# A written VectorE order for the expert loop, with gathered rows used a block later and the low half of the key rows made on VectorE

## The chip, the core and the metric

The kernel runs on one core of a Trainium2 chip, as one launch. The metric is device microseconds of one execution, from the start of the program to its end. The core has five engines that run side by side, each in the order of its own queue: TensorE (PE; its weight loads are shown apart as PEld), VectorE (DVE), ScalarE (ACT), GpSimd (POOL) and SyncE (SP), which here only issues DMA transfers. Engines wait for each other through semaphores.

## The reference

Two layers work on 512 tokens of width 1024 in float32. The first has chunked attention beside a state-space mixer, then attention over a memory of 256 rows; the second has dilated and differential attention. Each ends with the same kind of feed-forward part, a mixture of 16384 experts of one row each, and the change is in that part alone:

```python
def block(xb):                                   # 128 tokens
    q = (xb @ w_q).reshape(PEER_BLOCK, PEER_HEADS, 2, PEER_QDIM // 2)
    s = jnp.einsum('thsd,hsnd->thsn', q, sub_keys)
    sv, si = lax.top_k(s, PEER_TOPK)
    cand = sv[:, :, 0, :, None] + sv[:, :, 1, None, :]
    cidx = si[:, :, 0, :, None] * PEER_KEYS + si[:, :, 1, None, :]
    top, pos = lax.top_k(cand, PEER_TOPK)        # 16 experts for each of 8 heads
    e = jnp.take_along_axis(cidx, pos, axis=-1)
    g = jax.nn.softmax(top, axis=-1)
    act = gelu(jnp.einsum('thkd,td->thk', u_tab[e], xb))
    return jnp.einsum('thk,thkd->td', g * act, v_tab[e])
```

Each token thus uses 128 experts: for each, the dot product of a row of the table U (the key rows) with the token, its gelu times a gate, and that number times a row of the table V (the value rows), summed.

## The kernel before

Both layers call the same function `peer`; the first call has a side job, the second none. It treats the four token tiles of 128 in two ways.

**Three tiles are dense.** For them the gates of all 16384 experts are written out as a matrix (in device memory, `Gd`), and all experts are run as plain products in 128 blocks of 128 experts. For a block e, `pa` is the product of the key rows with the 384 tokens (24 matmuls of 384 columns), `ga` its gelu; `w` is `ga` times the block's gates, and `y` collects w times the value rows (18 matmuls of 512 columns into six accumulators). To keep float32 accuracy, each operand is split into a high half (a cast on ScalarE: `uh`, `vh`, `wh`) and a low half (the original minus the high half: `ul`, `vl`, `wl`), and three products stand for one. Key rows are loaded to `ur` and value rows to `vr`, 512 KB per block each, by SP; gates to `gbuf` for four blocks at a time.

**The fourth tile is gathered.** Row by row, for each of its 128 slots k, GpSimd issues an indirect DMA that fetches for each token its own key row (`urow`, L1229), and VectorE multiplies it with the token and sums (L1230, into `act`). Each 16 slots, ScalarE takes the gelu and VectorE multiplies with the gates (L1233, L1234). 32 slots later the value row is fetched (`vrow`, L1241) and added to `acc` with its weight (L1243). Both kinds of row have a pool of three buffers.

**The loop.** Products `pa` run 28 blocks ahead (`NA`): 28 of them are made before the loop, in the stages of routing and of writing the gates. Pass e of the loop emits: the load of `vr`; `vh` (L1262) and `vl` (L1263); `w`, `wh`, `wl` (L1267 to L1269); then `emit_A(e + 28)` (load of `ur`, `uh` L1099, `ul` L1105, `pa` L1112 to L1115, its gelu L1117); then a share of the list `ev` of the gathered tile's steps; then the matmuls of `y` (L1293 to L1295). From pass 100 on there are no `pa` products left and no gathers. There, in the first call only, the side job runs: the modulation of the second layer (three rows of it, 8 weight tiles `war` of 512 KB each, summed into `am` by VectorE, L823 and L825), two steps in each pass; and GpSimd makes `vl` in place of VectorE in passes 100 to 119. At pass 120 the gathered tile is finished.

**What sets the order.** The program is not run in the order in which it is written: a scheduler orders each engine's instructions when the kernel is compiled, by its own estimate of when each could start, and places the semaphores. `with tc.manual_schedule(engines={...})` takes this away: the instructions inside it, on the engines named, keep the order in which they are written. Before, that is so for GpSimd alone, around `emit_A` and the steps of `ev`. Low and high halves of values and weights, `vr`, `ur`, `uh` and `ul` have two buffers each, so work on a buffer of block e can start when block e-2 has let it go.

Of the kernel before, what the change touches and what calls it, by code (L numbers as in the profile page):

```python
# [8 lines left out]
F32 = mybir.dt.float32  # L9
# [14 lines left out]
def build(tc, I, out, dbg=None, stop=None):  # L24
# [28 lines left out]
    def rsqrt(ssq, n, scale, nm, eps=EPS):  # L53
        """1 / sqrt(ssq * scale + eps) for a [128, n] tile."""
# [24 lines left out]
    def transpose_split(src, ncol, hi, lo, dst, psum=None):  # L79
        """src [128, ncol*128] -> hi/lo[:, k, dst] for each 128-column chunk k."""  # L80
# [13 lines left out]
    def ssq_of(src, junk, nm):  # L94
        """sum of squares along the free axis on the scalar engine"""
        s = sm.tile([src.shape[0], 1], F32, name=nm, tag="ssq")
        A.activation(out=junk, in_=src, func=AF.Square, accum_out=s)
        return s
# [6 lines left out]
    def load_w(W, k, c0, cn, pool=None, e=V):  # L105
        """rows of chunk k of a weight matrix, as high and low halves"""
# [23 lines left out]
    def proj(hiT, loT, W, K, c0, cn, evac, tiles=range(NT), pool=None):  # L130
        """token-major product: for each token tile, psum[128, cn] = h @ W[:, c0:c0+cn]"""
# [16 lines left out]
    def keep_w(pool, W, K, c0, cn=512, last=0, e=V):  # L148
        """a block of weight columns on chip, for products of one token tile after the other"""
# [12 lines left out]
    def proj_rows(hiT, loT, ws, evac, then):  # L162
        """all token tiles in turn; then(t) follows two tiles behind"""
# [7 lines left out]
    # token order of everything after the first mixing: row p of tile r is token 4 p + r  # L171
# [6 lines left out]
    # =====================================================================  # L178
    # block 1: norm, input projection
    # =====================================================================  # L180
# [43 lines left out]
    def head_proj(pool, hi, lo, W, c0, nh, hd, tiles, finish, first=None, wait=False):  # L224
        """nh heads of width hd divided by their root mean square; finish(t, heads, scale)"""
# [92 lines left out]
    def cmul(o_r, o_i, a_r, a_i, b_r, b_i, pool, shape, conj_b=False, e=V):  # L318
        """o = a * b (or a * conj b)"""
# [22 lines left out]
    # powers a^0 .. a^8  # L342
# [14 lines left out]
    # c a^n: real part and negated imaginary part  # L357
# [16 lines left out]
    # unit phases e^{i Theta j}, Theta = 8 theta, and the decay of a chunk  # L374
# [37 lines left out]
    def coefficients():  # L412
        s5x = ExitStack()
        s5t = s5x.enter_context(tc.tile_pool(name="s5t", bufs=1, side="right"))
        # chunk-input coefficients, transposed to [(s, c), pair, (g2, p)]
# [12 lines left out]
        # block-Toeplitz matrices [(s, c_in), g, (t, c_out)], two groups of a pair at a time  # L428
# [94 lines left out]
    def norm_T(xt, gain, hi, lo, sl, pool, inplace=False, two=False):  # L523
        """rmsnorm of a [128, 1024] tile with gain, transposed and split"""
# [218 lines left out]
    def softmax_row(ps, n, z, pool, tag="pe"):  # L743
        """exp(scores - max) with its sum"""
# [43 lines left out]
    def modulation(rows, pool, psum, tags, ptag, on_pool):  # L788
        """rows of the modulation; yields after each block of 128 x 1024 weights"""
# [57 lines left out]
    EV = 100  # L847
# [6 lines left out]
    def queries(qp, Wq, hi, lo):  # L854
        """loads, halves and products of the 128-column blocks of the query weights"""
# [31 lines left out]
    def peer_route(rw, query, keysT, crep, E, GT, ahead, also, first):  # L887
        """expert indices (as float) and gates, [128, tile, 128 slots]

        Step l of 16 is one half of one head's query; the candidates of a head are  # L890
        looked up in the steps of the next head, and products of the first expert
        blocks run between the steps' products."""
# [23 lines left out]
        def top16(src, work, vals, idx, tiles):  # L916
            """the 16 largest of src[:, t] with their places, in order"""
# [152 lines left out]
    def peer(keysT_d, U, UT, Vt, front, finish, nm, side=None, also=None, then=None):  # L1070
# [49 lines left out]
        def emit_A(e):  # L1120
            a_dma(e)
            a_hi(e)
            a_lo(e)
            a_mm(e)
# [742 lines left out]
```

## Time and profile before

| | |
|---|---|
| three runs | 4092.52, 4095.1, 4101.62 us, median 4095.1 |
| span of the profiled execution, first to last instruction | 4090.4 us |
| PE busy | 3876.8 us, 95% |
| VectorE, GpSimd, ScalarE busy | 3004.6, 2145.8, 1654.8 us |
| the first expert loop | about 970 to 1960 us, its tail without `pa` from about 1807 on |
| the second expert loop | about 3116 to 4082 us, its tail from about 3958 on |

Lines such as L1263 are those of the kernel before. The profiled execution gives its span and not a time of its own beside it. PE's busy share counts pipelined matmuls, so the number of matmuls in a stretch tells more of its pace than the share does.

### The profile page before, as it was taken

The numbers are of one execution on the slowest core, as the hardware profiler recorded it, in microseconds if no ns is written. First come the engines' busy times: TensorE is split into PE (matmuls) and PEld (weight loads), VectorE is DVE, ScalarE is ACT, GpSimd is POOL, SyncE is SP. The second block draws the span as 40 slices with busy tenths as digits, with TensorE's granted clock in tenths as the row PEclk, the third lists the DMA queues.
The fourth block names the chain that finished last, engine by engine and source line by source line (L and its number), as shares of the span: only waits on it lengthen the run. The fifth ranks groups of instructions, "written<-read, shape, count | busy, mean of one in ns | idle before, by whom it ended". The sixth has DMA issues, their size and how long they took to land. (4 is left out here: it accounts for less than half of the span.)

```text
span 4090.4 us, 53234 instructions
## 1 busy us (share of the span) xinstructions
PE 3876.8 (95%) x19062; PEld 3370.2 (82%) x19062; DVE 3004.6 (73%) x5440; ACT 1654.8 (40%) x2567; POOL 2145.8 (52%) x1353
## 2 busy tenths in 40 slices
PE   6999998899999999989899988999899999999999
PEld 5777788899899999877777766788899899989887
DVE  8456489884787778777756566689884788878765
ACT  3454432454333333323444567332454333333333
POOL 3000057655777777754424433257655777776740
PEclk8999999999999999999999989999999999999999
DMA  3333132236898889986222323332237898888874
GB/s 112 99 111 106 52 113 79 101 134 230 302 319 320 315 311 315 318 275 221 90 81 57 93 75 100 102 114 79 98 134 250 299 322 314 311 306 308 299 254 150
DMA packets 330057, 784.31 MB, mean 192 GB/s; under 512 B 32048, under 2 KB 148864, under 8 KB 326400
## 3 DMA queue, kind: packets, MB, share of 16 engines
q1 hardware_dynamic: 252608, 499.86, 36.4%
q0 software_dynamic: 77184, 281.05, 19.5%
q8 instruction: 150, 2.46, 0.2%
q14 instruction: 115, 0.94, 0.1%
HBM read 722.98 MB, written 56.65 MB: 191 GB/s over the span
## 5 line engine op out<-in xcount | busy, mean ns | idle before, releaser
L1105 POOL TENSOR_TENSOR ul<-ur,uh 128x1024 fp32r<-128x1024 f32 x256 | 676.5, 2643 | 378.0 <-ACT uh L1099 259.5
L1112 PE MATMUL pa<-phi,uh 128*128 128x384 f32 x2048 | 695.5, 340 | 0.8 <-ACT ga L1117 0.8
L1113 PE MATMUL pa<-plo,uh 128*128 128x384 f32 x2048 | 694.8, 339 | 0.0
L1294 PE MATMUL y<-vl,wh 128*128 128x512 f32 x1536 | 606.2, 395 | 26.1 <-DVE vl L1263 22.4
L1295 PE MATMUL y<-vh,wl 128*128 128x512 f32 x1536 | 609.2, 397 | 11.3 <-DVE wl L1269 11.3
L1293 PE MATMUL y<-vh,wh 128*128 128x512 f32 x1536 | 603.8, 394 | 1.3 <-ACT wh L1268 1.2
L1243 DVE SCALAR_TENSOR_TENSOR acc<-vrow,act,acc 128x1024 f32<-128x1024 f32 x256 | 392.3, 1532 | 196.6 <-DMA vrow<-in_expert_v_dram,ei 99.5
L1230 DVE SCALAR_TENSOR_TENSOR urow<-urow,hgat 128x1024 f32<-128x1024 f32 x256 | 392.0, 1534 | 172.0 <-DMA urow<-in_peer_u_dram,ei 85.5
L1268 ACT CAST wh<-w 128x384 fp32r<-128x384 f32 x256 | 131.2, 513 | 736.0 <-PE y L1294 483.8
L1099 ACT CAST uh<-ur 128x1024 fp32r<-128x1024 f32 x256 | 269.3, 1052 | 382.9 <-PE pa L1113 149.2
L1115 PE MATMUL pa<-phi,ul 128*128 128x384 f32 x2048 | 402.5, 339 | 18.0 <-POOL ul L1105 17.9
L1112 PEld LDWEIGHTS pa<-phi,uh 128*128 128x128 f32 x2048 | 389.0, 190 | 10.0 <-ACT ga L1117 1.1
L1113 PEld LDWEIGHTS pa<-plo,uh 128*128 128x128 f32 x2048 | 389.1, 190 | 9.6
L1263 DVE TENSOR_TENSOR vl<-vr,vh 128x1024 fp32r<-128x1024 f32 x236 | 353.4, 1498 | 34.6 <-DMA ur<-in_peer_uT_dram 16.2
L1115 PEld LDWEIGHTS pa<-phi,ul 128*128 128x128 f32 x2048 | 362.0, 190 | 19.9 <-POOL ul L1105 19.9
L1206 PE MATMUL pgg<-oh,oh 128*128 128x128 f32 x1536 | 374.3, 421 | 4.4 <-DVE oh L1198 3.9
L1206 PEld LDWEIGHTS pgg<-oh,oh 128*128 128x128 f32 x1536 | 369.9, 337 | 7.1 <-issue 5.3
L1294 PEld LDWEIGHTS y<-vl,wh 128*128 128x128 f32 x1536 | 290.5, 189 | 93.5 <-DVE vl L1263 32.3
L1295 PEld LDWEIGHTS y<-vh,wl 128*128 128x128 f32 x1536 | 290.5, 189 | 85.0 <-DVE wl L1269 22.5
L1293 PEld LDWEIGHTS y<-vh,wh 128*128 128x128 f32 x1536 | 290.8, 189 | 55.5 <-ACT wh L1268 1.7
L77 DVE TENSOR_TENSOR wl<-wr,wh 128x512 fp32r<-128x512 f32 (+1 forms) x276 | 198.9, 729 | 148.9 <-ACT wh L76 148.8
L1200 POOL TENSOR_TENSOR oh<-oha,ohb 128x1024 f32<-128x1024 f32 x72 | 218.2, 3033 | 143.9 <-PE pgg L1206 104.5
(539 smaller groups left out, 7694.7 us busy)
## 6 DMA issues: line engine op xcount, KB each, us to landing
vr<-in_peer_v_dram SPq DMA_DIRECT2D x128, 512.0 KB
ur<-in_peer_uT_dram SPq DMA_DIRECT2D x128, 512.0 KB
vr<-in_expert_v_dram SPq DMA_DIRECT2D x128, 512.0 KB
ur<-in_expert_uT_dram SPq DMA_DIRECT2D x128, 512.0 KB
gbuf<-Gd SPq DMA_DIRECT2D x64, 768.0 KB
Gd<-stg SPq DMA_DIRECT2D x24, 1920.0 KB
wr<-in_w_in_dram SPq DMA_DIRECT2D x104, 256.0 KB
war<-in_w_ada_dram SPq DMA_DIRECT2D x24, 512.0 KB
```

The costliest lines, as they stand in the source:

```text
L1099: A.copy(out=uh, in_=ua[e])
L1105: G.tensor_tensor(out=ul, in0=raw, in1=uh.bitcast(F32), op=OP.subtract)
L1112: T.matmul(pa, uh[:, k, :], hi[:, k, 0:NDT], start=(k == 0), stop=False)
L1113: T.matmul(pa, uh[:, k, :], lo[:, k, 0:NDT], start=False, stop=False)
L1115: T.matmul(pa, ul[:, k, :], hi[:, k, 0:NDT], start=False, stop=(k == 7))
L1206: T.matmul(pg[:, j, :], oh2[:, :, 4 * q + j], oh1[:, :, 4 * q + j], start=True, stop=True)
L1230: V.scalar_tensor_tensor(out=row, in0=row, scalar=1.0, in1=hg_, op0=OP.mult, op1=OP.mult, accum_out=act[:, k:k + 1])
L1243: V.scalar_tensor_tensor(out=acc, in0=vrow.pop(k - 2), scalar=act[:, k - 2:k - 1], in1=acc, op0=OP.mult, op1=OP.add)
L1263: (G if side and EV <= e < EW else V).tensor_tensor(out=vl, in0=vr, in1=vh.bitcast(F32), op=OP.subtract)
L1293: T.matmul(y[t][c], wh[:, ts], vh[:, cs_], start=(e_ == 0), stop=False)
L1294: T.matmul(y[t][c], wh[:, ts], vl[:, cs_], start=False, stop=False)
L1295: T.matmul(y[t][c], wl[:, ts], vh[:, cs_], start=False, stop=(e_ == 127))
```

## The change

- The part under `manual_schedule` now holds VectorE's instructions too and begins earlier, so that VectorE's steps of a pass come in the written order: `w`, `vl`, `wl`, the uses of gathered rows, then `ul` of block e + 28. ScalarE's casts stand inside but stay with the scheduler; they are emitted as `wh`, `vh`.
- `emit_A(e + NA, V)` makes `ul` on VectorE instead of GpSimd in the loop's 100 passes. The 28 blocks before the loop keep GpSimd.
- A step of `ev` is now a pair of a fetch and a use. A pass uses the rows that the pass before fetched (`due`), and then fetches its own share. Before, a key row was used in the step that fetched it, and a value row two steps later. The 16-slot gelu is part of the last use of its 16. `ev` has 256 entries where it had 266, over the same 99 passes.
- `vl` is made on VectorE in all passes; GpSimd's share in passes 100 to 119 of the first call is gone.
- Comments are removed. Pools and buffer counts stay.

```diff
-        def a_lo(e):
+        def a_lo(e, eng=G):
             raw, uh = ua[e]
             ul = ub.tile([128, 8, 128], F32R, name="ul", tag="ul")
-            G.tensor_tensor(out=ul, in0=raw, in1=uh.bitcast(F32), op=OP.subtract)
+            eng.tensor_tensor(out=ul, in0=raw, in1=uh.bitcast(F32), op=OP.subtract)
...
-        def g_u(k):
-            row = gw.tile([128, 1024], F32, name="urow", tag="row")
-            G.indirect_dma_start(out=row, out_offset=None, in_=U, in_offset=bass.IndirectOffsetOnAxis(ap=ei[:, TL, k:k + 1], axis=0))
+        rows_ = {}
+
+        def u_in(k):
+            rows_[0, k] = gw.tile([128, 1024], F32, name="urow", tag="row")
+            G.indirect_dma_start(out=rows_[0, k], out_offset=None, in_=U, in_offset=bass.IndirectOffsetOnAxis(ap=ei[:, TL, k:k + 1], axis=0))
+
+        def u_use(k):
+            row = rows_.pop((0, k))
             V.scalar_tensor_tensor(out=row, in0=row, scalar=1.0, in1=hg_, op0=OP.mult, op1=OP.mult, accum_out=act[:, k:k + 1])
+            if k % 16 == 15:
+                k0 = k - 15
+                A.activation(out=act[:, k0:k0 + 16], in_=act[:, k0:k0 + 16], func=AF.Gelu)
+                V.tensor_tensor(out=act[:, k0:k0 + 16], in0=act[:, k0:k0 + 16], in1=GT[:, TL, k0:k0 + 16], op=OP.mult)
...
         ev = []
-        for k in range(128 + 34):
+        for k in range(128 + 32):
             if k < 128:
-                ev.append((g_u, k))
-                if k % 16 == 15:
-                    ev.append((g_w, k - 15))
+                ev.append((u_in, u_use, k))
             if k >= 32:
-                ev.append((g_v, k - 32))
+                ev.append((v_in, v_use, k - 32))
+        due = []
...
-            A.copy(out=vh, in_=vr)
-            (G if side and EV <= e < EW else V).tensor_tensor(out=vl, in0=vr, in1=vh.bitcast(F32), op=OP.subtract)
...
-            V.tensor_tensor(out=w.rearrange("p (a b) -> p a b", b=TG), in0=gbuf[:, :, e % EB, :], in1=gas.pop(e).rearrange("p (a b) -> p a b", b=TG), op=OP.mult)
-            A.copy(out=wh, in_=w)
-            V.tensor_tensor(out=wl, in0=w, in1=wh.bitcast(F32), op=OP.subtract)
-            with tc.manual_schedule(engines={mybir.EngineType.Pool}):
+            with tc.manual_schedule(engines={mybir.EngineType.Pool, DVE_}):
+                V.tensor_tensor(out=w.rearrange("p (a b) -> p a b", b=TG), in0=gbuf[:, :, e % EB, :], in1=gas.pop(e).rearrange("p (a b) -> p a b", b=TG), op=OP.mult)
+                A.copy(out=wh, in_=w)
+                A.copy(out=vh, in_=vr)
+                V.tensor_tensor(out=vl, in0=vr, in1=vh.bitcast(F32), op=OP.subtract)
+                V.tensor_tensor(out=wl, in0=w, in1=wh.bitcast(F32), op=OP.subtract)
+                for _, use, k in due:
+                    use(k)
                 if e + NA < 128:
-                    emit_A(e + NA)
+                    emit_A(e + NA, V)
                 want = min(len(ev), max(0, (len(ev) * (e + 1 - GS) + GE - 1) // GE))
-                while nev < want:
-                    f_, k_ = ev[nev]
-                    f_(k_)
-                    nev += 1
+                due = ev[nev:want]
+                nev = want
+                for get, _, k in due:
+                    get(k)
```

## Rows read from the trace of the kernel before

**Rows 1.** The page, busy time of each engine: us, share of the span, instructions.
```profile
PE 3876.8 (95%) x19062; PEld 3370.2 (82%) x19062; DVE 3004.6 (73%) x5440; ACT 1654.8 (40%) x2567; POOL 2145.8 (52%) x1353
```

**Rows 2.** Busy time by stretch: stretch and length; PE, PEld, DVE, ACT, POOL; PEclk, DMA share, GB/s.
```profile
970.00:1110.00 140.00, 134.75 (x668) 119.12 (x667) 96.62 (x124) 50.74 (x71) 94.39 (x56) 1.00 0.83 292
1110.00:1697.00 587.00, 587.00 (x2973) 534.18 (x2972) 478.84 (x496) 209.92 (x285) 437.59 (x254) 1.00 0.89 317
1697.00:1807.00 110.00, 106.08 (x527) 93.81 (x527) 77.25 (x72) 37.63 (x52) 80.22 (x45) 1.00 0.86 299
1807.00:1960.00 153.00, 134.54 (x581) 107.29 (x580) 117.56 (x130) 48.35 (x72) 58.40 (x24) 0.94 0.67 214
3116.00:3260.00 144.00, 139.97 (x694) 123.94 (x693) 100.52 (x128) 49.84 (x70) 97.69 (x59) 1.00 0.85 300
...
3587.00:3600.00 13.00, 10.12 (x42) 8.30 (x41) 13.00 (x14) 2.82 (x4) 7.37 (x5) 0.87 0.92 344
...
3790.00:3958.00 168.00, 163.51 (x812) 144.92 (x811) 122.72 (x122) 55.64 (x76) 117.10 (x69) 1.00 0.85 298
...
1933.00:1949.50 16.50, 16.50 (x73) 13.33 (x71) 8.24 (x17) 5.68 (x8) 0.00 (x0) 1.00 0.48 148
```

**Rows 3.** Waits of PE, 970 to 1110: us in total, times, longest us.
```profile
PE y L1294 <- DVE vl L1263: 5.2, 4, 2.5
```

**Rows 4.** Waits of DVE, 970 to 1110.
```profile
DVE urow L1230 <- DMA urow<-in_peer_u_dram,ei: 37.8, 16, 7.0
```

**Rows 5.** Waits of DVE, 1110 to 1697.
```profile
DVE acc L1243 <- DMA vrow<-in_peer_v_dram,ei: 59.7, 24, 6.1
```

**Rows 6.** Groups of POOL, 1110 to 1697: busy us, mean ns | idle before, releasers.
```profile
L1105 POOL TENSOR_TENSOR ul<-ur,uh 128x1024 fp32r<-128x1024 f32 x70 | 185.3, 2648 | 97.1 <-ACT uh L1099 92.4 <-PE pa L1115 2.5 <-issue 1.7
```

**Rows 7.** Timeline, 1306 to 1310: start, us, instruction [idle before <-releaser].
```profile
1306.48 1.21 DVE L1263 TENSOR_TENSOR vl<-vr,vh 128x1024 fp32r<-128x1024 f32 x1
...
1306.71 0.52 ACT L1268 CAST wh<-w 128x384 fp32r<-128x384 f32 x1 [3.45 <-PE y L1294]
...
1307.13 1.04 ACT L1262 CAST vh<-vr 128x1024 fp32r<-128x1024 f32 x1
...
1307.61 0.55 DVE L1269 TENSOR_TENSOR wl<-w,wh 128x384 fp32r<-128x384 f32 x1
...
1307.69 1.29 POOL L1229 DMA_INDIRECT urow<-in_peer_u_dram,ei  x1 [0.30 <-DVE vl L1263]
...
1308.08 1.21 DVE L1230 SCALAR_TENSOR_TENSOR urow<-urow,hgat 128x1024 f32<-128x1024 f32 x1
...
1309.48 0.86 PE L1115 MATMUL pa<-phi,ul 128*128 128x384 f32 x4
```

**Rows 8.** Timeline, 1311 to 1316.
```profile
1311.16 3.24 POOL L1105 TENSOR_TENSOR ul<-ur,uh 128x1024 fp32r<-128x1024 f32 x1 [0.58 <-ACT uh L1099]
...
1312.07 3.42 DVE L1263 TENSOR_TENSOR vl<-vr,vh 128x1024 fp32r<-128x1024 f32 x1
```

**Rows 9.** Timeline, 997.5 to 1004: a gather's issue and its use.
```profile
997.55 1.76 POOL L1229 DMA_INDIRECT urow<-in_peer_u_dram,ei  x1
...
1003.83 1.86 DVE L1230 SCALAR_TENSOR_TENSOR urow<-urow,hgat 128x1024 f32<-128x1024 f32 x1 [3.71 <-DMA urow<-in_peer_u_dram,ei]
```

**Rows 10.** Timeline, 3164 to 3175: a gather's issue and its use.
```profile
3164.43 1.76 POOL L1229 DMA_INDIRECT urow<-in_expert_u_dram,ei  x1 [0.15 <-issue]
...
3174.01 2.80 DVE L1230 SCALAR_TENSOR_TENSOR urow<-urow,hgat 128x1024 f32<-128x1024 f32 x1 [3.73 <-DMA urow<-in_expert_u_dram,ei]
```

**Rows 11.** Timeline, 1254 to 1261: a load of key rows and its cast.
```profile
1254.27 0.82 SPq L1094 DMA_DIRECT2D ur<-in_peer_uT_dram  x1
...
1260.62 1.05 ACT L1099 CAST uh<-ur 128x1024 fp32r<-128x1024 f32 x1 [2.21 <-DMA ur<-in_peer_uT_dram]
```

**Rows 12.** Timeline, 1318 to 1329: a load of key rows and its cast.
```profile
1318.23 1.02 SPq L1094 DMA_DIRECT2D ur<-in_peer_uT_dram  x1
...
1328.25 1.06 ACT L1099 CAST uh<-ur 128x1024 fp32r<-128x1024 f32 x1 [3.49 <-DMA ur<-in_peer_uT_dram]
```

More of the change, by code (lines that the diff above doesn't have):

```diff
@@ L1055, in build @@
     RG = (3, 6, 9, 11)
+    DVE_ = mybir.EngineType.DVE
     def peer_front(nm, Wq):
@@ L1118, in a_mm, with emit_A @@
             gas[e] = ga
-        def emit_A(e):
+        def emit_A(e, eng=G):
             a_dma(e)
             a_hi(e)
-            a_lo(e)
+            a_lo(e, eng)
             a_mm(e)
@@ L1225, in peer @@
         TL = ND
-        def g_u(k):
-            row = gw.tile([128, 1024], F32, name="urow", tag="row")
-            G.indirect_dma_start(out=row, out_offset=None, in_=U, in_offset=bass.IndirectOffsetOnAxis(ap=ei[:, TL, k:k + 1], axis=0))
-            V.scalar_tensor_tensor(out=row, in0=row, scalar=1.0, in1=hg_, op0=OP.mult, op1=OP.mult, accum_out=act[:, k:k + 1])
-        def g_w(k0):
-            A.activation(out=act[:, k0:k0 + 16], in_=act[:, k0:k0 + 16], func=AF.Gelu)
-            V.tensor_tensor(out=act[:, k0:k0 + 16], in0=act[:, k0:k0 + 16], in1=GT[:, TL, k0:k0 + 16], op=OP.mult)
@@ L1236, in peer @@
-        vrow = {}
-        def g_v(k):
-            if k < 128:
-                vrow[k] = gw.tile([128, 1024], F32, name="vrow", tag="vrow")
-                G.indirect_dma_start(out=vrow[k], out_offset=None, in_=Vt, in_offset=bass.IndirectOffsetOnAxis(ap=ei[:, TL, k:k + 1], axis=0))
-            if k >= 2:
-                V.scalar_tensor_tensor(out=acc, in0=vrow.pop(k - 2), scalar=act[:, k - 2:k - 1], in1=acc, op0=OP.mult, op1=OP.add)
-        ev = []
-        for k in range(128 + 34):
-            if k < 128:
-                ev.append((g_u, k))
-                if k % 16 == 15:
-                    ev.append((g_w, k - 15))
+        rows_ = {}
@@ new lines, in v_in, with v_use @@
+        def v_in(k):
+            rows_[1, k] = gw.tile([128, 1024], F32, name="vrow", tag="vrow")
+            G.indirect_dma_start(out=rows_[1, k], out_offset=None, in_=Vt, in_offset=bass.IndirectOffsetOnAxis(ap=ei[:, TL, k:k + 1], axis=0))
+        def v_use(k):
+            V.scalar_tensor_tensor(out=acc, in0=rows_.pop((1, k)), scalar=act[:, k:k + 1], in1=acc, op0=OP.mult, op1=OP.add)
+        ev = []
+        for k in range(128 + 32):
+            if k < 128:
+                ev.append((u_in, u_use, k))
```

## The prediction

> **What bounds the kernel now.** I read the page's busy line first: TensorE (PE) is busy 95% of the span [rows 1], so only two kinds of change can move the time: fewer matmul microseconds (none here) or fewer holes in PE. Next come the stretches of the two expert loops [rows 2]. In 1110 to 1697 PE has no hole: 2973 matmuls in 587 us, 5.065 per us, and with 42 matmuls in a block (24 of `pa`, 18 of `y`) a block lasts 8.29 us. A stretch that holds fewer matmuls than 5.065 per us has lost the rest. By that count 970 to 1110 lost 140 - 668/5.065 = 8.1 us, 1697 to 1807 lost 6.0, 3116 to 3260 lost 7.0, 3587 to 3600 lost 4.7 and 3790 to 3958 lost 7.7. These are 33.5 us. 1807 to 1960 is the tail of the first loop, without `pa`; there the undisturbed rate is 73 in 16.5 us, 4.42 per us, so 581 matmuls are worth 131 us of 153 and 22 are lost. (Some records are missing from a trace, so each of these is good to about 1 us.)
>
> What PE waits for is seen in its waits: in the first of these stretches it is `vl`, VectorE's low half of the value rows [rows 3]. Why `vl` is late is seen in VectorE's own waits: 37.8 us in 16 waits for gathered rows in 140 us [rows 4]. VectorE executes in order, and its order before lets a use of a gathered row stand ahead of `vl`. The full stretch has such waits too (59.7 us for `vrow` alone [rows 5]), but there they stay hidden. The gathers start late because GpSimd makes `ul` between them, and `ul` stood 92.4 us waiting for ScalarE's `uh` [rows 6], with the next gathers queued behind it.
>
> **The change, part by part.** One block in detail [rows 7]: `wh` starts when the previous `y` products end (1306.71), the same moment at which PE turns to `pa`; `vh` follows 0.42 later; a 1024-wide VectorE step lasts 1.21 and its successor starts 1.13 after it; a 384-wide one takes 0.47.
>
> (1) *`ul` goes from GpSimd to VectorE*: 100 blocks per loop, 1.13 us each on VectorE (same shape and types as `vl`). What goes away is the clash: a VectorE step beside a `ul` on GpSimd lasts 3.42 instead of 1.21 [rows 7, 8], about once per block, so 2.2 us. VectorE's load was 478.84 us in 587 [rows 2], 6.76 per block. After: `w` 0.47, `vl` 1.13, `wl` 0.47, 2.59 row uses (256 in 99 blocks) at about 1.16 = 3.0, `ul` 1.13, in all 6.2 of 8.29. VectorE does not become the bound by load.
>
> (2) *The written order* `w, vl, wl, uses, ul`. Counted from the end of `y` of block e-2: `vh` done at 1.5, `vl` 1.56 to 2.7, `wl` to 3.2, uses to 6.2, `ul` done at 7.4. `vl` is wanted only when `y(e)` begins, at about 12.4, so it has 9 us of cover where a row wait ahead of it now used that up. `ul(e+28)` is wanted by the last third of its `pa`: one block later plus 2.77 (L1115 starts at 1309.48 [rows 7]), that is 11.06. Its cover is 3.7 us. This is the new weak point: everything VectorE waits for in the list delays `ul`, and the load of the key rows two blocks on, which needs the same buffer, is issued on SP only after it. VectorE can catch up 2 us per block.
>
> (3) *Rows used a block later.* GpSimd's queue in the loop then holds only gathers, each waiting just for its buffer of three. From issue to use a row took 6.3 us at one end [rows 9] and 9.6 at the other [rows 10]; with 1.21 of use and some 0.2 of wake-up a buffer turns round in 7.7 to 11.0 us. Where u and v rows alternate, a buffer is wanted only every 3/1.29 blocks = 19 us: no waits at all, so the 4.7 us at 3587 should go (I leave 1). Where only u rows (first 12 blocks) or only v rows (last 12) run, it is wanted every 3/2.59 blocks = 9.6 us. At 7.7 nothing waits; at 11.0 each of 10.7 turns lags 1.4, 15 in all less the cover of 3.7, so 11 us lost. The middle, 9.35, just fits, and only three-row blocks in succession lag; I take 2.5 us for each of the four phases, with 0 and 11 as ends. They lost 8.1, 7.0, 6.0 and 7.7: 28.8 becomes 10, gain 18.8. The mid stretch gives 3.7.
>
> (4) *Tail of the first loop*: `vl` of blocks 100 to 119 returns to VectorE (20 x 1.13 = 23 us), against clashes that go. The modulation steps of L825 are not in the written order and still stand between VectorE's other work, which fills 117.56 of the 153 us there [rows 2]. Ends: nothing gained, or 15 of the 22; I take 7, near the middle. The second loop's tail keeps its order of work; nothing.
>
> (5) *New costs.* Each 16th u use is now followed at once by ScalarE's gelu and a product on VectorE: 16 round trips which may stand behind a `uh`, each up to 3 us and so within the cover; 0.3 each, 5 in all (ends 0 and 16). In block 0 `w` stands ahead of `vl` and waits for its gate block: under 1 us, in the same figure. SP's order of loads otherwise only follows. Making `vl` after `wh` on ScalarE costs nothing, with the 9 us as cover.
>
> Sum: 18.8 + 3.7 + 7 - 5 = 24.5 us. On the profiled execution, span 4090.4, that is 4066; the median of the three runs, 4095.1, stands 4.7 above that span, so 4071. The difference that a measurement of this kernel can tell from none is 0.2%, 8.2 us.
>
> A rule that speaks against it: the Trainium skill, "SBUF — State Buffer", section "SBUF: two separate sides", warns that GpSimd cannot write the descriptors of the DMAs it issues while a VectorE step in a two-port mode holds the port pair that they share. The trace shows a gather's issue of 1.29 us starting at 1307.69 right through `wl` and the use after it, none of them longer than elsewhere [rows 7]; so here I give it little.
>
> **The rivals.**
> *The key-row ring* (slower). Load of `ur`, `uh`, then, if ScalarE has `uh` queued ahead of the next `wh` and `vh`, the whole list down to `ul`, then the next load in that buffer: X + 1.05 + 7.4 us per two blocks, X from load issue to `uh`. It decides above 16.58, X over 8.1. X was 6.4 in one place [rows 11] and 10.0 in another [rows 12]. Were X 9 on average, a block would last (17.45 - 16.58) / 2 = 0.43 us longer, over some 194 blocks 84 us: 4071 + 84 = 4155. At 8.4 it is 0.13 x 194 = 26, so 4097, and at 10 it is 4252. For it: `uh` was already held up by its load in both [rows 11, 12]. Against: in the written order the loads of value rows and of key rows leave SP some 5 us apart (`vl` done at 2.7, `ul` at 7.4), so that one queues less behind the other.
> *Stalls only change their owner*: the four phases lose 7 each as now (ring near 10 us) and the tail gains nothing: 4095 - 3.7 + 5 = 4096. For it: rows already lay 6 to 10 us before use, which is about a block.
> *Descriptors starve*, by the mechanism that the rule gives: a gather's issue waits out a 1.2 us step, the ring grows to 8.9 to 12.2 (middle 10.5): lag 0.9 x 10.7 - 3.7 = 6 per phase, 14 us less gain: 4085.
> *All holes close*, tail included at its upper end: 4095 - 33.5 - 15 = 4047.
>
> **How the numbers follow.** Forecast 0.56 (its own range 4055 to 4086), all holes close 0.05, ring 0.19, changed owner 0.13, descriptors 0.05, something else that costs time 0.02. Range 4048 to 4125: it leaves out the half of the ring with X above 8.7 (0.10), the lower half of the case with all holes closed and the unnamed costs. Faster by over 0.2%: 0.56 + 0.05 + 0.02 of the descriptors = 0.63; within 0.2%: owner 0.13, the mildest of the ring 0.03, the rest of the descriptors 0.03, so 0.19; slower: 0.16 of the ring and 0.02, so 0.18.
>
> **What would show it.** Right: in the alternating stretch VectorE waits for rows almost vanish, PE has no hole there, no VectorE step of 3.4 us before the tail, and the losses by count in the four phases are about 2 to 3 each. Wrong: PE waiting for `ul` (L1105) all through the loop, blocks longer than 8.29 us with `uh` released by the `ur` load (the ring); row waits of the old size in the four phases (owner); gather issues longer than 1.8 us (descriptors).

## The result

The changed kernel takes 4043.3 us (median of 4 runs, 4033.0 to 4049.5), the kernel before in the same comparison 4093.8 (4080.0 to 4101.6): a ratio of 0.9887, 95% interval 0.9859 to 0.9915, so 46 us (35 to 58) faster. The forecast was 24.5 us, to 4071, with a range from 4048: the direction was right, the size about half, and the time lies 5 us under the range.

The busy line of the changed kernel's page (profiled execution 4044.2 us, span 4042.4), to be read beside [rows 1]: the same matmuls in a shorter span, and GpSimd (POOL) 559 us less busy.

```profile
PE 3858.9 (95%) x19062; PEld 3364.5 (83%) x19062; DVE 2935.5 (73%) x5660; ACT 1634.6 (40%) x2567; POOL 1586.4 (39%) x1133
```

Busy time by stretch, same columns as [rows 2]; they are shifted with the loops: the first loop starts 5 us earlier than before, the second 30.

```profile
966.00:1105.00 139.00, 134.49 (x665) 120.54 (x665) 97.92 (x142) 48.74 (x70) 52.77 (x39) 0.99 0.87 298
1105.00:1692.00 587.00, 587.00 (x2974) 534.20 (x2973) 450.17 (x565) 204.14 (x288) 265.07 (x184) 1.00 0.91 317
1692.00:1800.00 108.00, 105.36 (x534) 95.39 (x533) 80.32 (x86) 34.79 (x51) 38.12 (x30) 1.00 0.86 290
1800.00:1938.00 138.00, 131.93 (x583) 104.77 (x582) 106.44 (x155) 49.49 (x74) 6.21 (x5) 0.98 0.73 242
3086.00:3230.00 144.00, 143.59 (x723) 129.81 (x724) 106.37 (x152) 49.77 (x72) 56.41 (x42) 1.00 0.92 316
3747.00:3915.00 168.00, 167.22 (x847) 151.64 (x846) 127.78 (x145) 56.25 (x80) 66.11 (x48) 1.00 0.87 299
3915.00:4034.00 119.00, 118.77 (x523) 97.66 (x521) 71.93 (x96) 40.05 (x55) 5.42 (x4) 1.00 0.54 163
```

Counted as in the prediction (5.065 matmuls per us, 4.42 in a tail), what TensorE loses went at the head of the first loop from 8.1 to 7.7 us, at its end from 6.0 to 2.6, in its tail from 22 to 6.1, at the head of the second loop from 7.0 to 1.3 and at its end from 7.7 to 0.8. A second profile of each kernel (below) gives, in the same order without the tail, 7.3, 7.3, 6.0 and 8.9 us before and 2.2, 1.6, 1.3 and none after; so the 7.7 that is left at the first head belongs to one profile.

What is left is read from the waits between 966 and 1110 (us in total, times, longest us), beside [rows 3, 4]. L1116 is the last third of `pa`, L1273 `vl`, L1237 the use of a u row, L1100 `uh`, L1095 the load of `ur`:

```profile
PE pa L1116 <- DVE ul L1106: 4.4, 4, 2.2
PE y L1299 <- ACT wh L1271: 0.9, 1, 0.9
...
DVE vl L1273 <- ACT vh L1272: 22.8, 8, 5.5
DVE urow L1237 <- DMA urow<-in_peer_u_dram,ei: 15.8, 9, 3.6
...
ACT uh L1100 <- DMA ur<-in_peer_uT_dram: 69.0, 13, 8.9
...
SPq L1095 <- DVE ul L1106: 78.6, 17, 9.5
```

`vl` is no longer what TensorE waits for; it is `ul`, and behind it a circle: SP holds the load of the next key rows until `ul` has freed their buffer, and ScalarE's `uh` waits for that load. Row waits in this stretch fell from 37.8 to 15.8 us. In the full stretch, 1105 to 1692, VectorE's waits are these two and none is for a row ([rows 5] had 59.7 us for `vrow`):

```profile
DVE vl L1273 <- ACT vh L1272: 131.2, 68, 4.6
DVE act L1241 <- ACT act L1240: 4.9, 2, 2.9
```

One block of it (start, us, instruction), beside [rows 7, 8]: `vl` in 1.23 us and no step of 3.4 us any more; a gather issues in 1.67 and 1.31 us beside VectorE's steps; `vl`'s first use by TensorE comes in the block that starts at 1323.17.

```profile
1307.27 1.67 POOL L1245 DMA_INDIRECT vrow<-in_peer_v_dram,ei  x1 [2.79 <-DVE acc L1248]
1308.06 1.23 DVE L1106 TENSOR_TENSOR ul<-ur,uh 128x1024 fp32r<-128x1024 f32 x1
...
1309.25 1.31 POOL L1233 DMA_INDIRECT urow<-in_peer_u_dram,ei  x1 [0.30 <-issue]
...
1309.31 0.33 SPq L1095 DMA_DIRECT2D ur<-in_peer_uT_dram  x1
...
1312.39 1.23 DVE L1273 TENSOR_TENSOR vl<-vr,vh 128x1024 fp32r<-128x1024 f32 x1 [2.64 <-ACT vh L1272]
...
1316.21 1.05 ACT L1100 CAST uh<-ur 128x1024 fp32r<-128x1024 f32 x1 [3.85 <-DMA ur<-in_peer_uT_dram]
```

### The profile page after: what moved, and what is told of

It is laid out like the page before. It is cut to its first block, busy times and chain, and to the rows that moved or that the text cites. A ratio compares the mean times of both kernels' runs of the same rounds, so it can differ in the third digit from the quotient of the medians.

```text
span 4042.4 us, 53263 instructions
## 1 busy us (share of the span) xinstructions
PE 3858.9 (95%) x19062; PEld 3364.5 (83%) x19062; DVE 2935.5 (73%) x5660; ACT 1634.6 (40%) x2567; POOL 1586.4 (39%) x1133
## 5 line engine op out<-in xcount | busy, mean ns | idle before, releaser
L1100 ACT CAST uh<-ur 128x1024 fp32r<-128x1024 f32 x256 | 269.5, 1053 | 921.4 <-DMA ur<-in_peer_uT_dram 427.8
L1273 DVE TENSOR_TENSOR vl<-vr,vh 128x1024 fp32r<-128x1024 f32 x256 | 313.4, 1224 | 407.6 <-ACT vh L1272 407.6
L1301 PE MATMUL y<-vh,wl 128*128 128x512 f32 x1536 | 601.1, 393 | 0.8 <-DVE wl L1274 0.8
L1116 PE MATMUL pa<-phi,ul 128*128 128x384 f32 x2048 | 407.4, 342 | 27.4 <-POOL ul L1106 17.4
L1116 PEld LDWEIGHTS pa<-phi,ul 128*128 128x128 f32 x2048 | 364.4, 191 | 33.2 <-POOL ul L1106 19.4
L1248 DVE SCALAR_TENSOR_TENSOR acc<-vrow,act,acc 128x1024 f32<-128x1024 f32 x256 | 327.4, 1279 | 18.8 <-DMA vrow<-in_peer_v_dram,ei 10.0
L1237 DVE SCALAR_TENSOR_TENSOR urow<-urow,hgat 128x1024 f32<-128x1024 f32 x256 | 310.8, 1219 | 28.8 <-DMA urow<-in_peer_u_dram,ei 15.8
L1245 POOL DMA_INDIRECT vrow<-in_expert_v_dram,ei x128 | 192.4, 1503 | 241.7 <-DVE acc L1248 209.0
L1245 POOL DMA_INDIRECT vrow<-in_peer_v_dram,ei x128 | 191.4, 1496 | 234.5 <-DVE acc L1248 206.7
L1272 ACT CAST vh<-vr 128x1024 fp32r<-128x1024 f32 x256 | 267.7, 1047 | 29.1 <-DMA vr<-in_peer_v_dram 29.1
```

Of the source, the lines that this page charges most:

```text
L1100: A.copy(out=uh, in_=ua[e])
L1116: T.matmul(pa, ul[:, k, :], hi[:, k, 0:NDT], start=False, stop=(k == 7))
L1237: V.scalar_tensor_tensor(out=row, in0=row, scalar=1.0, in1=hg_, op0=OP.mult, op1=OP.mult, accum_out=act[:, k:k + 1])
L1245: G.indirect_dma_start(out=rows_[1, k], out_offset=None, in_=Vt, in_offset=bass.IndirectOffsetOnAxis(ap=ei[:, TL, k:k + 1], axis=0))
L1248: V.scalar_tensor_tensor(out=acc, in0=rows_.pop((1, k)), scalar=act[:, k:k + 1], in1=acc, op0=OP.mult, op1=OP.add)
L1273: V.tensor_tensor(out=vl, in0=vr, in1=vh.bitcast(F32), op=OP.subtract)
```

## The experiments

The change has four parts: the **order** written down for VectorE (without it the planner, the scheduler that orders instructions at compile time, chooses), rows used a block **later**, `ul` on **VectorE**, and `vl` on VectorE also in passes 100 to 119 (the **tail** part). Each kernel below takes away one part or two, or alters one detail. Times vary by some 0.3% from run to run, so besides the ratio to the kernel before (95% interval) I read from each profiled execution how long the two expert loops took, from their first `y` product to their last, tails included, and of that the first loop's tail (from the last `pa` product on). The last column is the rest of the program up to the second loop, where the order of instructions is the same in all of them.

| kernel | us | ratio | loops, us | tail 1 | outside |
|---|---|---|---|---|---|
| before (two profiles) | 4093.8 | | 1954.7, 1959.5 | 153.4, 154.5 | 2126.8, 2117.1 |
| changed (two profiles) | 4043.3 | 0.9887 (0.9859 to 0.9915) | 1919.6, 1908.6 | 138.1, 138.3 | 2114.2, 2113.6 |
| changed without order | 4173.3 | 1.0219 (1.0194 to 1.0243) | 2038.9 | 128.1 | 2115.4 |
| changed, `ul` on GpSimd | 4034.1 | 0.9883 (0.9861 to 0.9906) | 1900.1 | 134.5 | 2107.7 |
| changed without tail part | 4059.4 | 0.9941 (0.9917 to 0.9964) | 1926.8 | 146.3 | 2138.7 |
| before, `ul` on VectorE | 4363.8 | 1.0678 (1.0650 to 1.0706) | 2231.0 | 130.3 | 2127.2 |
| order and tail part alone | 4043.1 | 0.9898 (0.9872 to 0.9924) | 1916.0 | 137.9 | 2124.8 |
| changed, rows in their own block | 4060.7 | 0.9940 (0.9914 to 0.9965) | 1936.4 | 133.3 | 2118.8 |
| later and tail part alone | 4045.6 | 0.9925 (0.9904 to 0.9946) | 1917.7 | 139.2 | 2116.7 |
| changed, six row buffers shared | 4041.2 | 0.9899 (0.9866 to 0.9933) | 1908.0 | 137.4 | 2119.8 |
| the same, `ul` on GpSimd | 4025.0 | 0.9856 (0.9830 to 0.9882) | 1898.1 | 135.0 | 2122.1 |
| changed, `ul` ahead of the rows | 4030.3 | 0.9878 (0.9858 to 0.9898) | 1903.9 | 136.3 | 2115.9 |

The kernel before took 4080 to 4083 us beside the kernels from the third row on, on other chips; so ratios are compared between the rows of the table, not times. (All the first tails hold the same 521 `y` matmuls. In the two slow kernels, the third row and the sixth, the planner had moved the modulation steps of L825 out of the tail into the loop, to 1544 to 1611 and 1649 to 1713; their tails are shorter for that, so tails are compared only among the fast ones.)

**How much is variation.** Both kernels were profiled a second time.

> The kernel before once more, for a second profile. The time outside the expert loops (start to the first value product, and from the end of the first loop's tail to the second loop) was 2126.8 us in the first profile of the kernel before and 2114.2 in that of the changed one; its instruction order is the same in both. Theory 1 (that difference of 12.6 us is variation between executions): the second profile lies anywhere between 2108 and 2139, as ten other profiles of kernels with the same order there do, while the two loops with their tails take 1954.7 us again within 4. Theory 2 (the change makes the rest of the program faster): 2125 to 2129 us.

> The changed kernel once more, for a second profile. Theory 1 (variation between executions): outside the loops anywhere between 2108 and 2139 us, the two loops with their tails 1919.6 us within 4. Theory 2 (the change makes the rest faster): outside the loops 2112 to 2116 us.

The single times of these two executions were 4087.4 and 4032.6 us. Outside the loops they took 2117.1 and 2113.6 us. The first lies outside the range of theory 2; the second lies in both ranges and decides nothing. All 14 profiles lie between 2107.7 and 2138.7 without regard to the parts that they hold. So the 12.6 us by which the first pair of profiles differ there is mostly variation and no gain of the change. In the loops the kernel before came back within 5 us (4 had been expected), the changed one only within 11: the two blocks that stalled on `ul` at 1768 and 3408 were 2.4 and 3.2 us longer than 8.29 in the first profile, 1.9 and 0.5 in the second. I take the means, 1957.1 and 1914.1: the loops gained 43 us, and a single profile's sum of the loops is good to some 10 us.

**Without the written order.** Edit, at the list of VectorE's work:

```
-            with tc.manual_schedule(engines={mybir.EngineType.Pool, DVE_}):
+            with tc.manual_schedule(engines={mybir.EngineType.Pool}):
```

> The changed kernel with one part undone: VectorE's order in the expert stream is again left to the planner; the key rows' low halves stay on VectorE, the gathered rows stay a block later, and the value rows' low halves stay on VectorE in passes 100 to 119. Theory 1 (the written order is the main part): vl falls behind uses of rows that have not landed, and the stalls of the expert loops come back for the most part, some 20 of the 35 us that the loops gained: about 4063 us. Theory 2 (taking GpSimd's subtraction away is the main part, since it frees the gather queue and VectorE's port): the loops stay as in the changed kernel, about 4045 us.

Not 20 but some 125 us come back: slower than the kernel before. The written order is needed; but as the loss is far above the whole gain, something else in the change must make it necessary.

**`ul` back on GpSimd, and `ul` alone on VectorE.** The first edit is on the changed kernel, the second (with `a_lo` and `emit_A` taking the engine, as in the change) on the kernel before:

```
-                    emit_A(e + NA, V)
+                    emit_A(e + NA)
```

```
-                    emit_A(e + NA)
+                    emit_A(e + NA, V)
```

> The changed kernel with one part undone: the key rows' low halves are made on GpSimd again; order and rows a block later stay. Theory 1 (order): vl still stands ahead of the rows, so TensorE loses only what the slower subtraction costs where ul is last; 3.24 us instead of 1.13 and the clash of 2.2 us on VectorE in each block, still within VectorE's room of 2.1 us a block: 4043 to 4055 us. Theory 2 (ul is the main part): most of the gain goes, about 4080 us.

> The kernel before with one part of the change: only the key rows' low halves go to VectorE. Theory 1 (order): VectorE, in the planner's order, still runs vl behind rows that have not landed; the clash of 2.2 us a block goes and gathers are issued earlier, which is worth a few us: about 4083 us. Theory 2 (ul is the main part): 4055 us or less.

Neither theory foresaw either. With `ul` on GpSimd the loops are not slower but some 14 us faster (1900.1 against 1908.6 and 1919.6; by ratio, 0.9883 against 0.9887, the two can't be told apart). Its waits of PE, 966 to 1110, its full stretch, 1110 to 1697 (columns as in [rows 2]), and its groups of `ul`, `vl`, u row uses and `w` there (busy us, mean ns | idle before); the last line is the u row uses of the changed kernel, 1105 to 1692:

```profile
PE y L1300 <- DVE vl L1273: 1.1, 1, 1.1
PE pa L1116 <- POOL ul L1106: 0.4, 1, 0.4
```

```profile
1110.00:1697.00 587.00, 587.00 (x2974) 534.21 (x2973) 528.65 (x500) 213.60 (x290) 474.90 (x256) 1.00 0.91 319
```

```profile
L1106 POOL TENSOR_TENSOR ul<-ur,uh 128x1024 fp32r<-128x1024 f32 x72 | 214.3, 2976 | 62.4 <-ACT uh L1100 61.6 <-issue 0.2
L1273 DVE TENSOR_TENSOR vl<-vr,vh 128x1024 fp32r<-128x1024 f32 x71 | 95.1, 1339 | 56.5 <-ACT vh L1272 28.0 <-ACT wh L1271 27.0 <-issue 1.5
L1237 DVE SCALAR_TENSOR_TENSOR urow<-urow,hgat 128x1024 f32<-128x1024 f32 x93 | 159.1, 1711 | 0.8 <-DMA urow<-in_peer_u_dram,ei 0.8
L1270 DVE TENSOR_TENSOR w<-gbuf,ga 128x384 f32<-128x384 f32 x72 | 94.6, 1314 | 0.0
```

```profile
L1237 DVE SCALAR_TENSOR_TENSOR urow<-urow,hgat 128x1024 f32<-128x1024 f32 x91 | 110.8, 1217 | 0.0
```

The clash with GpSimd is back: VectorE is busy 528.65 of 587 us instead of 450.17, although it has no `ul` to make, which took 88.3 us of the 450.17. The clash thus costs it some 167 us, 2.4 per block, and most of that falls on the row uses (1.71 us instead of 1.22) and on `w` (1.31 instead of 0.55). `ul` takes 2.98 us and stands behind `uh` for 61.6 us as in [rows 6], and TensorE loses nothing by all this. VectorE's room was enough; what the subtraction costs on either engine is not the question here, but what it stands behind.

`ul` alone on VectorE, in the planner's order, costs 280 us. Its waits of PE and its stretch, 1110 to 1697; then one stall (DVE uses rows, makes `wl`, uses a row, makes `vl`, while PE stands), and the stretches before, in and behind that stall:

```profile
PE y L1294 <- DVE vl L1263: 90.5, 36, 5.1
```

```profile
1110.00:1697.00 587.00, 493.36 (x2245) 428.18 (x2244) 439.84 (x528) 159.14 (x221) 250.81 (x198) 0.92 0.89 311
1400.00:1404.00 4.00, 4.00 (x18) 3.31 (x19) 4.00 (x7) 0.00 (x0) 2.06 (x2) 1.00 0.81 268
1408.50:1413.40 4.90, 0.04 (x1) 0.00 (x0) 4.05 (x6) 1.44 (x2) 0.88 (x1) 0.86 0.47 176
1413.50:1418.50 5.00, 5.00 (x12) 3.94 (x13) 5.00 (x7) 0.00 (x0) 4.09 (x4) 0.50 0.82 261
```

```profile
1409.35 1.22 DVE L1230 SCALAR_TENSOR_TENSOR urow<-urow,hgat 128x1024 f32<-128x1024 f32 x1 [4.31 <-DMA urow<-in_peer_u_dram,ei]
...
1412.17 1.22 DVE L1263 TENSOR_TENSOR vl<-vr,vh 128x1024 fp32r<-128x1024 f32 x1
...
1413.44 0.79 PE L1294 MATMUL y<-vl,wh 128*128 128x512 f32 x1 [4.89 <-DVE vl L1263]
```

A row that came 4.31 us late stood ahead of `vl`, TensorE stood 4.89 us, and then it ran at a granted clock of 0.50 (1.2 GHz) for 5 us more: 12 matmuls where the stretch before the stall had 18 in 4 us. At the full rate those 12 would have taken 2.7 us, so the stall cost about half as much again as it lasted. 2245 matmuls in 587 us are 10.98 us per block.

The cover of `vl`, from its end to the first product that reads it, tells these kernels apart. Medians over the blocks of 1110 to 1697, worked out from the trace: before 2.95 us; `ul` alone on VectorE 0.05; changed without order 0.33; later and tail part alone 3.31; order and tail part alone 8.39; changed 9.96; changed with `ul` on GpSimd 9.95. The planner, given `ul` as one more step of VectorE, placed rows and `ul` so that `vl` became ready only when it was wanted; why it did is not in the trace. ScalarE's order of casts is no rival: it is `uh`, gelu, `wh`, `vh` in all but one or two blocks of this stretch in every kernel.

**Order alone, later alone.** Two kernels with `ul` on GpSimd and the tail part: in one VectorE's order is written and each row is used in the block that fetches it, in the other rows are used a block later and the planner orders. In the first the lines that use the rows become (`ul` and fetches stay in GpSimd's order):

```
+                if e + NA < 128:
+                    emit_A(e + NA)
                 want = ...
...
+                for get, use, k in due:
+                    get(k); use(k)
```

> VectorE's written order alone: key rows' low halves on GpSimd, and each gathered row used in the block that fetches it, behind w, vl and wl of that block; value rows' low halves on VectorE in passes 100 to 119 as in the changed kernel. Theory 1 (the order is the part that pays, and a block later adds nothing, because a gather starts when a row buffer comes free, whatever block its line stands in): the two loops stay within 4 us of those with rows a block later (825.4 and 821.5 us from the first value product to the last key-row product), about 4035 us in all. Theory 2 (the prediction's step: a row must have 9.6 us from fetch to use, which only a block later gives): the waits for rows of 3 to 4 us come back, each loop is 10 us or more longer, 4055 us or more.

> The changed kernel with two parts undone: VectorE's order is the planner's again and the key rows' low halves are on GpSimd again; rows a block later and the value rows' low halves on VectorE in passes 100 to 119 stay. The two loops with their tails took 1954.7 us in the kernel before and 1900.1 with the written order beside these parts. Theory 1 (the written order is what pays, rows a block later only add to it): 1940 us or more, 4070 us in all. Theory 2 (the later use alone lets the planner put the rows behind vl): 1915 us or less, 4045 us in all.

My first theory fell in the second of these and half in the first. Either part alone, with the tail part, brings about 40 us (1916.0 and 1917.7 against 1957.1), both together 57 (1900.1). Of that 18, 16 and 24 us lie in the two tails; ahead of the tails it is 22.8 us by order, 23.9 by the later use and 32.7 by both. So the two don't add. That they are two ways to one end, fewer uses of late rows ahead of `vl`, is borne out in part. Before, VectorE has two row uses right ahead of `vl` in 29 blocks of each loop and one in 68; with order alone it has none in 85 to 88, and the cover of `vl` rises to 8.39 us; with the later use alone it has two in 6 and one in some 90, but the cover stays at 3.31 and VectorE still waits 32.7 us for u rows at the first head (37.8 before). How the later use alone saves as much is therefore not fully shown. PE waits, 966 to 1110, of order alone and of later alone:

```profile
PE y L1301 <- DVE wl L1274: 3.7, 2, 2.1
PE y L1300 <- DVE vl L1273: 0.3, 1, 0.3
```

```profile
PE y L1300 <- DVE vl L1273: 2.8, 2, 1.5
```

The third way round, the changed kernel with rows in their own block (fetch and use, then `ul` on VectorE):

```
...
+                for get, use, k in due:
+                    get(k); use(k)
                 if e + NA < 128:
                     emit_A(e + NA, V)
```

> The changed kernel with one part undone: each gathered row is used in the block that fetches it, behind w, vl and wl and ahead of the key row's low half; VectorE's written order and both subtractions on VectorE stay. Theory 1 (a block later adds nothing): within 5 us of the changed kernel, 4038 to 4048 us. Theory 2 (a block later gives the gathers their time): VectorE waits 3 to 4 us more in many blocks, and with the key row's low half behind those waits TensorE stalls on it: 4060 us or more.

4060.7 us, at the second theory's bound: the later use is worth some 22 us in the loops there (1936.4 against 1914.1). Ahead of the tails nothing is left of the gain: 841.3 and 842.9 us for the two loops, 840.4 and 839.3 before. But the later use does not pay by giving a gather more time. From a gather's issue to its use, median over the 128 rows of each kind and loop, it is 15.4 to 15.8 us in this kernel as in the changed one; 7.9 to 8.2 in the kernel before and with later alone; 7.6 to 7.8 with order alone; 10.9 to 11.5 with order and later and `ul` on GpSimd. So under the written order the lead follows from what else stands in GpSimd's queue, not from the block in which the line of the use stands. In the planner's order a queue without `ul` is not enough: without order the lead is 9.8 to 9.9 us, with `ul` alone on VectorE 7.5 to 12.1. What the later use does shorten is the wait for `ul`: PE's waits for it over both loops were 22.7 us here and 9.9 and 2.7 in the changed kernel's two profiles. At the worst place the circle is seen again: a key-row load issued at 1078.94 let `uh` start only at 1092.43, 13.5 us later, `vl` waited 10.38 us for the `vh` queued behind that `uh`, and TensorE waited 4.66 us for `ul` at 1101. Why a use one block earlier tightens the circle is left open.

**`ul` ahead of the rows.** The changed kernel with the two steps swapped:

```
+                if e + NA < 128:
+                    emit_A(e + NA, V)
                 for _, use, k in due:
                     use(k)
-                if e + NA < 128:
-                    emit_A(e + NA, V)
```

> The changed kernel with one pair swapped in VectorE's written order: the key row's low half stands ahead of the uses of gathered rows, not behind them. Its move to VectorE has cost about 20 us (1919.6 us for the two loops with their tails, against 1900.1 with it on GpSimd). Theory 1 (it costs that because it stands behind uses that wait for rows, so that the key row's buffer comes free late, its load is issued late and ScalarE, waiting for that load, makes the next vh late): most of the 20 us comes back, 1900 to 1906 us, about 4028 us in all. Theory 2 (it costs that because VectorE then waits for the key row's high half in front of everything else): no better than the changed kernel or worse, 1919 us or more, 4043 us in all.

The first theory's number came: 1903.9 us, ratio 0.9878. PE, ACT and SP, 966 to 1110:

```profile
PE pa L1116 <- DVE ul L1106: 0.2, 1, 0.2
...
ACT uh L1100 <- DMA ur<-in_peer_uT_dram: 14.3, 5, 5.5
...
SPq L1095 <- DVE ul L1106: 24.2, 18, 3.9
```

SP holds the load 24.2 us instead of 78.6, `uh` waits for it 14.3 instead of 69.0, TensorE 0.2 instead of 4.4. Over both loops TensorE waited for `ul` 9.9 and 2.7 us in the changed kernel's profiles, 10.3 without the tail part, 3.8 with six buffers shared and 22.7 with rows in their own block, all with `ul` last; 0.4 with `ul` ahead of the rows and at most 0.4 with `ul` on GpSimd. So `ul` at the end of the list cost what it did through the circle of the key rows' buffer, and its place, not its engine, was the fault. (By ratio alone, 0.9878 against 0.9887, the two kernels can't be told apart, and the loops differ by 5 to 16 us, in part variation; the waits carry this.)

**More row buffers.** Rows of both kinds take the two sets of three buffers by turns, so that six serve a stretch that fetches one kind; on the changed kernel, and with `ul` on GpSimd (`u_in` and `v_in` take the set as an argument):

```
+                for i, (get, _, k) in enumerate(due, nev):
+                    get(k, ("row", "vrow")[i % 2])
                 nev = want
```

> The changed kernel with the row buffers dealt out by turns to both kinds of rows, so that a stretch in which only one kind is fetched has six buffers and not three. Theory 1 (the stalls that are left stand where one kind is fetched, since three buffers give a gather less time than it takes): the 18 us that TensorE still loses at the heads and ends of the two loops fall to under 8, about 4033 us. Theory 2 (the row's wait there is the transfer's own time, or VectorE's, and more buffers don't help): loss as in the changed kernel, 4043 us.

> The changed kernel with the key rows' low halves on GpSimd again and the six row buffers dealt out by turns to both kinds of rows. If the key row's low half, standing last on VectorE behind the rows, is what still stalls TensorE, the version with it on GpSimd has nothing left that more buffers can give: within 3 us of 4034 us. If rows waited for in the single-kind stretches still cost there, 4028 us or less.

On the changed kernel 1908.0 us lies between nothing and 12 us gained, which is inside its own variation, though VectorE's 15.8 us of waits for rows at the first head went. With `ul` on GpSimd the median, 4025.0 us, meets the number that was named for row waits (4028 or less), but the loops change by only 2 us and its ratio, 0.9856 against 0.9883, is within the intervals; so that theory is not borne out, and this fastest kernel of all can't be told from its neighbours. The three buffers were not what bound.

**The tail part.**

```
-                V.tensor_tensor(out=vl, in0=vr, in1=vh.bitcast(F32), op=OP.subtract)
+                (G if side and EV <= e < EW else V).tensor_tensor(out=vl, in0=vr, in1=vh.bitcast(F32), op=OP.subtract)
```

> The changed kernel with one part undone: in passes 100 to 119 of the first expert loop the value rows' low halves are made on GpSimd again. Theory A (that move made the gain in the tail, where before lost 27 us and after 13): the time from the last key-row product to the last value product goes from 138 us back to about 150, 4055 us in all. Theory B (the order of w, wl and the rows made it): that time stays within 2 us, 4043 us in all.

Between the theories, nearer the first: the tail takes 146.3 us, 8 more than in the changed kernel's profiles and 8 less than before. That does not make the written order a second half of the gain: with the later use and the tail part alone, in the planner's order, the tail took 139.2 us, 14.8 less than before (the two profiles of a kernel agree here within about 1 us, and the gathers, and so the later use, end where the tail begins). So either of the two shortens the tail, and the return of `vl` to VectorE by itself nearly all the way. In the kernel before, PE waits of 1800 to 1900 and VectorE at 1822 (L825 is the modulation step, L1269 `wl`):

```profile
PE y L1295 <- DVE wl L1269: 8.1, 3, 5.7
PE ptmod L806 <- DVE bada L803: 3.3, 1, 3.3
PE y L1294 <- POOL vl L1263: 3.1, 2, 1.9
```

```profile
1822.19 3.29 DVE L825 SCALAR_TENSOR_TENSOR am<-war,cc,am 128x1024 f32<-128x1024 f32 x1 [0.34 <-DMA war<-in_w_ada_dram]
1825.40 0.55 DVE L1269 TENSOR_TENSOR wl<-w,wh 128x384 fp32r<-128x384 f32 x1
```

and without the tail part, then in the changed kernel, in the same stretch, then with later and tail part alone, 1801 to 1940 (the tails begin at 1807, 1814, 1800 and 1801):

```profile
PE y L1300 <- POOL vl L1273: 5.0, 4, 2.6
PE y L1301 <- DVE wl L1274: 4.1, 2, 3.0
```

```profile
PE y L1299 <- ACT vh L1272: 2.0, 4, 1.0
PE pmod L800 <- DVE rxh L59: 1.5, 1, 1.5
PE y L1300 <- DVE vl L1273: 0.5, 1, 0.5
```

```profile
PE y L1300 <- DVE vl L1273: 7.8, 7, 5.1
```

Before, a 3.29 us modulation step stood ahead of `wl`, and TensorE waited for `wl` and for GpSimd's `vl`. The longest L825 is 3.3 us in both profiles of the kernel before and 3.4 without the tail part, where GpSimd makes `vl`; it is 1.3 in the changed kernel and with later and tail part alone, where it does not.

## Why the prediction was right and wrong

The sign and the place were right: TensorE's holes lay in the expert loops where `vl` stood behind rows, and they closed. By stage, means of two profiles each: first loop up to its last `pa` product 840.4 to 830.5, its tail 154.0 to 138.2, second loop 839.3 to 826.8, its tail 123.5 to 118.7. That is 9.9 + 15.8 + 12.5 + 4.8 = 43.0, against 24.5 forecast. With it the forecast would have been 4052, inside the range; the remaining 9 us to 4043.3 lie outside the loops, where the profiles differ by 8 on the mean, and that is within variation. So it is chance that the time fell under the range, but not that the gain was taken at little more than half its size.

*The sum's largest miss is the tails* (20.6 measured, 7 forecast). This is the step that failed: term (4). For the first tail I took 7 us for the return of `vl` to VectorE, near the middle of 0 and 15. The return is worth 14.8 us in the planner's order (with rows a block later), and 8 only on top of the written order, which without it brings 7.7; I had counted the modulation steps as standing in the way all the same, but without GpSimd's `vl` beside them they lasted 1.3 us and not up to 3.4. For the second tail I put nothing, because it keeps its order of work. It did not: before, TensorE lost 4.7 us in the block at 3962, where `vl` stood behind the last two v rows and the four steps that finish the gathered tile. The tail was 123.5 us then and is 118.7 now.

*The loops* (22.4 measured, 17.5 forecast) were close. The four phases kept 7.7 + 2.6 + 1.3 + 0.8 = 12.4 us in one profile and about 5 in the other, where I left 10, but not for the reason given: three row buffers were to lag, and six changed the loops by 2 us where `ul` was on GpSimd; what was left at the first head was `ul`. The 4.7 us at 3587 were a single stall: the second profile of the kernel before has none there, but one of 3.4 us at 1580.

*Step 1* called the clash of 2.2 us per block a thing that goes. It went (`vl` 1.23 us; 2.4 us per block in all), and in the loops it was worth nothing: with the clash back, TensorE lost less. VectorE's load was never the bound, as the same step says, and the sum rightly has no price for the clash there. What it lacks is a price for the move of `ul`: ahead of the tails, order and later use with `ul` left on GpSimd gain 32.7 us, and with `ul` moved 22.4.

*Step 2* was the best one. `vl` was given 9 us of cover and has 9.96; `ul` was named the new weak point with 3.7 us, and it is what TensorE still waits for. But I let its cost pass into other terms; the loops give 5 to 16 us for its place behind the rows, in part variation, and the written list could have had it ahead of them for nothing.

*Step 3* put the gathers' time under the wrong part. A block later is not what gives a gather its time: later alone left the lead at 8 us. With the written order, taking `ul` out of GpSimd's queue raised it to 15.5, as the step's own reason, a queue of gathers alone, would have it; yet the longer lead bought nothing, since the loops were shorter with `ul` on GpSimd and a lead of 11. And the turns of 7.7 to 11.0 us per buffer were read from a kernel in which that queue still held `ul`.

*Step 5*, gelu round trips: VectorE waited 4.9 us for them in two waits of the full stretch. One at 3408 was longer than the 3 us that I allowed and than the cover of `ul`: 5.55 us, because the gelu stood behind a `uh` that waited for its load. The block lasted 3.2 us longer there, and in the other profile, where that wait was 4.07, 0.5. The new costs of 5 us came in part:

```profile
3409.20 1.05 ACT L1100 CAST uh<-ur 128x1024 fp32r<-128x1024 f32 x1 [7.70 <-DMA ur<-in_expert_uT_dram]
...
3410.40 0.17 DVE L1241 TENSOR_TENSOR act<-act,GT 128x16 f32<-128x16 f32 x1 [5.55 <-ACT act L1240]
...
3412.96 1.51 PE L1116 MATMUL pa<-phi,ul 128*128 128x384 f32 x4 [1.86 <-DVE ul L1106]
```

*The rivals.* The key-row ring, to which I gave 0.19, is real and had its signs all through (`uh` waited for its load 284.5 us in 66 waits of 1105 to 1692, against 45.3 in 16 before) but stayed below its point of decision in the full stretch: the load shown above took 6.9 us from issue to cast (1309.31 to 1316.21) and the median of the stretch is 6.4, under the 8.1 from which blocks grow, and 2974 matmuls in 587 us are the same 8.29 us per block. Where it bit, mostly at the heads and ends, it cost a few us. Stalls that only change their owner: in part true at the head of the first loop in one profile, 8.1 to 7.7 us with `ul` in place of `vl`; 2.2 in the other. Descriptors: the sign that I named, issues longer than 1.8 us, came in 51 of 512 gathers (19 before), but none was longer than some 2.0 us in either kernel and the mean rose only from 1.35 to 1.41, far from the 1.2 us more that the rival needs; so the trace speaks against it. All holes closed, 4047 with 0.05, was nearest to what happened; it took the first tail at its upper end, 15, where 15.8 were measured.

The Trainium skill, "Perfetto Trace Analysis", section "Optimizing Scalar/DVE Operations", says that moving operations between GpSimd and VectorE might not help, since they share an SBUF read port. The trace agrees on the clash (a mean of 1.71 us for a u row use with `ul` on GpSimd, 1.22 without) and adds that the move changed the time by its place in the queue: from 280 us lost to some 6 us from the best, for one and the same step on VectorE.

## What to carry to other kernels

Where an engine runs in order, price a moved step by what stands ahead of it and what waits behind it, not by its duration: `ul` on VectorE cost 280 us in one order, about 14 in another and 4, which is within variation, in a third. Put the steps that feed TensorE and those that free a buffer for a load ahead of anything that waits for a gather, and check the cover of each. Two parts of a change that cure one stall don't add; take one away at a time, in both directions, before calling a part the gain.

## What the runs showed of the hardware

After a stall of 4.89 us TensorE's granted clock was 0.50 for the next 5 us, and in the kernel with such stalls all through the loop it was 0.92 over 587 us, against 1.00 in the kernel before and in the changed one; so such a hole cost about half as much again as it lasted. A clash of VectorE's steps with GpSimd's subtraction that cost VectorE some 167 us in 587 (a u row use 1.71 us instead of 1.22, `w` 1.31 instead of 0.55) cost TensorE nothing there; in the first tail, where GpSimd's `vl` went with modulation steps of up to 3.4 us instead of 1.3, the tail was 8 us longer with it. The part of the program that no edit touched took between 2107.7 and 2138.7 us in 14 profiles: 31 us, more than the effect of most single parts here, which is why the loops were compared by themselves.
